# Wide gate products, 512-wide matmuls first, and three attention projection tiles placed among the gates

## The chip, the cores and the metric

The kernel runs on one core of a Trainium2 chip. The metric is the device time of one execution in microseconds. TensorE is called PE below, VectorE DVE, ScalarE ACT, GpSimd POOL, and SyncE, which issues most of the loads, SP. PE multiplies a stationary block of weights (128x128) with a moving block of up to 512 columns into a PSUM bank (128 x 512 fp32, eight banks).

## The reference

A two-layer encoder over 512 tokens of width 1024, in fp32. Per layer, with `h = rms_norm(x)`:

```python
z = h @ w_in[l]
q, k, v, cb, cc, cx, ga, gb = jnp.split(z, splits, axis=-1)
y_attn = band_attention(q, k, v, attn_sink[l]) @ w_attn_proj[l]
y_conv = (cb * short_conv(cc * cx, conv_w[l])) @ w_conv_proj[l]
mix = (jax.nn.sigmoid(ga) * y_attn + jax.nn.sigmoid(gb) * y_conv) @ w_out[l]
x = x + rms_norm(mix, g_post_mix[l])
h = rms_norm(x, g_pre_ffn[l])
f = (jax.nn.silu(h @ w_gate[l]) * (h @ w_up[l])) @ w_down[l]
x = x + rms_norm(f, g_post_ffn[l])
```

The change touches the gates `ga`, `gb` (two 1024x1024 products with h), the two projections that they weigh, the merge, and the order of matmuls in the gate and up products of the feed-forward block (FFN, 2816 wide).

## The kernel before, in words

**Precision.** Each fp32 operand is split into a high part (a cast to fp32r on ACT) and a low part (source minus high part, a subtraction on DVE). A product is the sum of three matmuls, high by low, low by high, high by high (`mm3`, L181 to L184). Some splits go "by DMA" instead (`split_by_dma`, L134): ACT writes the high part and the negated high part, and a DMA issued by POOL adds the source to it, so DVE does nothing.

**Stages of a layer**, in the order in which PE runs them: the value, key and query projections with the attention's pieces, interleaved with the conv branch; the conv projection (8 tiles, L856); the attention projection (8 tiles of 24 matmuls 512 wide, L933 to L938); the gates; w_out (`down`, L275, 8 blocks of k, five of them kept for the last pass); the FFN's gate and up products; w_down.

**Pairs.** Gates and FFN products are computed by `Pair` (L416): two output tiles (weights w0, w1, 1024 x 128 each) times the whole h, as 7 products of half size (a Strassen and Winograd scheme) instead of 8. A product p has four k steps. Its weight block is a sum of halves of the two weight tiles, made by DVE and then split (`prep`, L439). Its moving operand is one of seven sums of quarters of h, 256 columns high part and 256 low part, side by side. In the narrow form a k step is `mm3` with three 256-wide matmuls. In the wide form (`wide`, L502 and L506) a k step is one 512-wide matmul, high weights by both parts at once, and one 256-wide, low weights by the high part; the high-by-low sum then lies in the second half of the bank and is added when the bank is read (`total` L536, `plus` L544, and L528). Before the change all gates and the first five FFN pairs are narrow, and the other 17 FFN pairs are wide.

**What sets the order.** `orders` (L558) makes the list of (pair, product); `run_pairs` (L595) walks it, asking for the weights of the next 10 entries, making the operands of the next 5 (`AHEAD`) and those that go by DMA of the next 8 (`FAR`). Each engine runs its own instructions in order, and SP issues its loads in order, each when its destination is free. Buffers are taken in rotation: 22 slots of 4 KB per partition (`unit`, tag u4: second weight tiles, q, kept results, sums of h), 3 raw tiles (first weight tiles), 8 `hl` tiles (split weights), 6 each of t4 and t2, 8 PSUM banks.

**Gates.** `Gates.first` (L914) applies the sigmoid and multiplies by the attention's projection `ya`; `Gates.second` (L918) does the other gate with the conv projection `yc`, adds both, and splits the sum for w_out at once (L924 to L926). `yc` is kept in u4 slots from the conv projection on (L858 to L861), as is half of `ya`.

## Time and profile before

| what | value |
|---|---|
| median of 3 runs | 1645.69 us (1645.08 to 1647.68) |
| the profiled execution | 1645.89 us |
| its span | 1644.1 us, 25284 instructions |
| mean granted TensorE clock | 0.999 |
| attention projection, layer 0 | 312.7 to 356.3 us |
| gates, layer 0 | 356.3 to about 437 us |
| wide FFN pairs, layer 0 | about 541.5 to 703.3 us |

The span is what the profiler saw from the first to the last instruction; the execution's own time is 1.8 us longer. Rows of groups and of the timeline name the source line, the engine, the operation, and the tiles out<-in without their buffer numbers, so `bank<-u,hl` is a matmul that reads a moving operand in a u4 slot and a split weight tile.

### The profile page before, as it was taken

The page shows a single profiled execution, that of the slowest core. Times are in us where ns is not written, and L with a number is a line of the kernel's source. Part 1 is how long each engine was busy: PE and PEld are TensorE (multiplying, and loading weights), DVE is VectorE, ACT ScalarE, POOL GpSimd, SP SyncE. Part 2 cuts the span into 40 slices and gives each one's busy share as a digit, 9 for nine tenths or more (in the row PEclk, how much of TensorE's full clock was granted, in tenths as well). Part 3 has the DMA queues.
Part 4 walks back from the last instruction along what each step waited for, and adds up shares of the span by engine and source line. Part 5 has one row for each costly group of instructions (what it writes and reads, how often), then busy time and mean ns, then how long its engine had stood idle before and what let it go on. Part 6 is the DMA issues. An engine that isn't in the chain of part 4 may idle for free. (4 is left out here: it accounts for less than half of the span.)

```text
span 1644.1 us, 25284 instructions
## 1 busy us (share of the span) xinstructions
PE 1632.1 (99%) x9119; PEld 1422.5 (87%) x9119; DVE 1258.4 (77%) x2563; ACT 984.3 (60%) x2102; POOL 159.0 (10%) x222
## 2 busy tenths in 40 slices
PE   9999999999999999999999999999999999999998
PEld 8888888889989888888898888888998898888886
DVE  6978876749769999964469788766696799999442
ACT  5566666547657677743346676664575677777331
POOL 0000000000013222200000000000010332222000
PEclk9999999999999999999999999999999999999999
DMA  6322222245575766734413222223457657666332
GB/s 210 91 77 78 64 78 77 84 119 127 166 208 113 161 155 162 182 117 142 149 57 103 78 78 77 78 67 88 102 143 211 170 125 170 159 157 164 103 115 77
DMA packets 264541, 200.58 MB, mean 122 GB/s; under 512 B 7216, under 2 KB 238688, under 8 KB 264416
## 3 DMA queue, kind: packets, MB, share of 16 engines
q1 hardware_dynamic: 246240, 171.70, 35.4%
q0 software_dynamic: 17600, 26.22, 9.6%
q8 instruction: 71, 1.16, 0.3%
q10 hardware_dynamic: 576, 1.05, 0.2%
q14 instruction: 54, 0.44, 0.1%
HBM read 164.34 MB, written 8.39 MB: 105 GB/s over the span
## 5 line engine op out<-in xcount | busy, mean ns | idle before, releaser
L131 ACT CAST hl<-raw 128x512 fp32r<-128x512 f32 x362 | 220.9, 620 | 237.3 <-PE bank L184 181.9
L132 DVE TENSOR_TENSOR hl<-raw,hl 128x512 fp32r<-128x512 f32 x362 | 244.6, 688 | 154.4 <-ACT hl L131 154.0
L182 PE MATMUL bank<-h,hl 128*128 128x512 f32 (+1 forms) x992 | 340.1, 343 | 2.2 <-DVE h L214 2.2
L183 PE MATMUL bank<-h,hl 128*128 128x512 f32 (+1 forms) x992 | 336.5, 339 | 0.0
L184 PE MATMUL bank<-h,hl 128*128 128x512 f32 (+1 forms) x992 | 336.1, 339 | 0.0
L182 PEld LDWEIGHTS bank<-h,hl 128*128 128x128 f32 x992 | 188.3, 190 | 21.3 <-DVE h L214 3.5
L184 PEld LDWEIGHTS bank<-h,hl 128*128 128x128 f32 x992 | 188.1, 190 | 20.8
L183 PEld LDWEIGHTS bank<-h,hl 128*128 128x128 f32 x992 | 188.3, 190 | 17.6
L502 PE MATMUL bank<-h,hl 128*128 128x512 f32 x544 | 195.4, 399 | 0.0
L182 PE MATMUL bank<-u,hl 128*128 128x256 f32 (+1 forms) x568 | 189.4, 334 | 0.0
L184 PE MATMUL bank<-u,hl 128*128 128x256 f32 (+1 forms) x568 | 188.2, 331 | 0.0
L183 PE MATMUL bank<-u,hl 128*128 128x256 f32 (+1 forms) x568 | 188.1, 331 | 0.0
L132 DVE TENSOR_TENSOR hl<-t,hl 128x512 fp32r<-128x512 f32 x240 | 165.9, 695 | 18.8 <-ACT hl L131 17.6
L131 ACT CAST hl<-t 128x512 fp32r<-128x512 f32 x240 | 147.8, 621 | 33.5 <-DVE t L452 13.9
L506 PE MATMUL bank<-h,hl 128*128 128x256 f32 x544 | 152.8, 281 | 0.0
L502 PE MATMUL bank<-u,hl 128*128 128x512 f32 x408 | 147.3, 399 | 0.0
L502 PEld LDWEIGHTS bank<-h,hl 128*128 128x128 f32 x544 | 102.2, 188 | 25.2
L183 PE MATMUL bank<-hl,u 128*128 128x512 f32 x304 | 118.3, 389 | 0.0
L184 PE MATMUL bank<-hl,u 128*128 128x512 f32 x304 | 118.3, 389 | 0.0
L184 PEld LDWEIGHTS bank<-u,hl 128*128 128x128 f32 x568 | 107.9, 190 | 10.2
L182 PE MATMUL bank<-hl,u 128*128 128x512 f32 x304 | 116.6, 390 | 0.0
L182 PEld LDWEIGHTS bank<-u,hl 128*128 128x128 f32 x568 | 107.9, 190 | 10.0
(155 smaller groups left out, 3195.7 us busy)
## 6 DMA issues: line engine op xcount, KB each, us to landing
raw<-in_w_in_dram SPq DMA_DIRECT2D x88, 512.0 KB, 3.8
u<-in_w_up_dram SPq DMA_DIRECT2D x44, 512.0 KB, 6.7
raw<-in_w_down_dram SPq DMA_DIRECT2D x44, 512.0 KB, 3.4
raw<-in_w_gate_dram SPq DMA_DIRECT2D x40, 512.0 KB, 4.1
hl<-u POOLq DMA_DIRECT2D x58, 256.0 KB, 4.3
hl<-raw POOLq DMA_DIRECT2D x34, 256.0 KB, 3.7
raw<-in_w_conv_proj_dram SPq DMA_DIRECT2D x16, 512.0 KB, 3.7
raw<-in_w_attn_proj_dram SPq DMA_DIRECT2D x16, 512.0 KB, 3.8
```

Source lines behind the costliest of these rows:

```text
L131: nc.scalar.copy(h, raw)
L132: eng.tensor_tensor(out=lo, in0=raw, in1=h.bitcast(F32), op=ALU.subtract)
L182: nc.tensor.matmul(acc, wh, xl, start=first, stop=False, skip_group_check=goes_on)
L183: nc.tensor.matmul(acc, wl, xh, start=False, stop=False, skip_group_check=goes_on)
L184: nc.tensor.matmul(acc, wh, xh, start=False, stop=last, skip_group_check=goes_on)
L502: nc.tensor.matmul(acc.rearrange("p (a t) -> p a t", a=2), hl[:, 0, k], x, start=new and k == 0, stop=False, skip_group_check=True,)
L506: nc.tensor.matmul(acc[:, :TH], hl[:, 1, k], x[:, 0], start=False, stop=k == KH - 1, skip_group_check=True)
```

## The change

Five edits:

1. In a wide product all four 512-wide matmuls come first, then the four 256-wide. This holds for the wide FFN pairs and for the gates.
2. The gates are wide, and the weights of products 4, 2 and 1 are split by DMA (before: of product 4 alone).
3. The first five tiles of the attention projection stay ahead of the gates; tiles 5, 6 and 7 come before entries 20, 32 and 44 of the gates' list, as objects of a class `Projected` that count as two tiles in the look-ahead.
4. The conv projection's result goes to DRAM (8 stores of 256 KB a layer) and is loaded back in four loads of 512 KB, each issued at product 2 of an even gate.
5. From the third gate on, the merged result is kept in fp32 and split when w_out needs it.

Core of the diff:

```diff
         def product(self, p):
...
             acc = self.b if p == 2 else self.c if p in (5, 3) else self.a
             hl, op, new = self.hl.pop(p), self.r.op(p), p in (2, 1, 5)
+            wide = acc.shape[-1] == T
+            if wide:
+
+                for k in range(KH):
+                    nc.tensor.matmul(
+                        acc.rearrange("p (a t) -> p a t", a=2), hl[:, 0, k], row_of(op, k),
+                        start=new and k == 0, stop=False, skip_group_check=True,
+                    )
             for k in range(KH):
                 x = row_of(op, k)
-                if self.wide:
-                    nc.tensor.matmul(
-                        acc.rearrange("p (a t) -> p a t", a=2), hl[:, 0, k], x,
-                        start=new and k == 0, stop=False, skip_group_check=True,
-                    )
+                if wide:
                     nc.tensor.matmul(
                         acc[:, :TH], hl[:, 1, k], x[:, 0], start=False, stop=k == KH - 1, skip_group_check=True
                     )
...
-            for j, q in seq[n : n + FAR]:
-                if q in pairs[j].by_dma:
-                    pairs[j].prep(q)
-            for j, q in seq[n : n + AHEAD]:
-                pairs[j].prep(q)
+            for far in (True, False):
+                left = FAR if far else AHEAD
+                for j, q in seq[n : n + FAR]:
+                    left -= pairs[j].tiles
+                    if left < 0:
+                        break
+                    if not far or q in pairs[j].by_dma:
+                        pairs[j].prep(q)
             pairs[i].product(p)
...
+    merge_seq = []
+    for n, item in enumerate(orders(KT, 2, 3)):
+        tiles = range(5) if n == 0 else [5 + (n - 20) // 12] if n >= 20 and (n - 20) % 12 == 0 else []
+        merge_seq += [(KT + m, 0) for m in tiles if m < KT] + [item]
...
         def conv_proj(m):
             acc = yield from gemm_steps(a["w_conv_proj"][l], m * P, lambda k, part: cy[k][:, part])
-            if m % 2 == 0:
-                held["yc"] = unit([P, 2, T], F32)
-            yc[m] = held["yc"][:, m % 2]
-            nc.scalar.copy(yc[m], acc)
+            y = t2([P, T])
+            nc.scalar.copy(y, acc)
+            nc.sync.dma_start(ycd[l][:, m], y)
...
+        class Projected:
+            by_dma, tiles = (), 2
...
+            def product(self, p):
+                m = self.m
+                if m % 2 == 0:
+                    held["ya"] = unit([P, 2, T], F32)
+                ya[m] = held["ya"][:, m % 2]
+                acc = bank()
+                for k in range(KT):
+                    mm3(acc, self.hl(0, k), self.hl(1, k), qs[k][:, 0], qs[k][:, 1], k == 0, k == KT - 1)
+                nc.scalar.copy(ya[m], acc)
+
+        def parts_of(x):
+            u = unit([P, 2, T])
+            split_to(u[:, 0], u[:, 1], x)
+            return u[:, 0], u[:, 1]
+
         class Gates(Pair):
-            by_dma = (4,)
+            by_dma, wide = (4, 2, 1), True
+
+            def product(self, p):
+                super().product(p)
+                m = self.m
+                if p == 2 and m % 2 == 0:
+                    u = unit([P, 2, T], F32)
+                    nc.sync.dma_start(u, ycd[l][:, m : m + 2])
+                    yc[m], yc[m + 1] = u[:, 0], u[:, 1]
...
                 nc.vector.tensor_tensor(out=out, in0=out, in1=yc[m], op=ALU.mult)
-                nc.vector.tensor_tensor(out=out, in0=out, in1=self.out0, op=ALU.add)
-                u = unit([P, 2, T])
-                split_to(u[:, 0], u[:, 1], out)
-                mix[m] = u
+                if m < SOON:
+                    nc.vector.tensor_tensor(out=out, in0=out, in1=self.out0, op=ALU.add)
+                    mix[m] = parts_of(out)
+                    return
+                if (m - SOON) % 2 == 0:
+                    held["mix"] = unit([P, 2, T], F32)
+                mix[m] = held["mix"][:, (m - SOON) % 2]
+                nc.vector.tensor_tensor(out=mix[m], in0=out, in1=self.out0, op=ALU.add)
...
-        run_pairs(gates, gate_seq)
+        run_pairs(gates + [Projected(m) for m in range(KT)], merge_seq)
...
             down(
-                a["w_out"][l], KT, 5, lambda k: (mix[k][:, 0], mix[k][:, 1]), after_mix,
+                a["w_out"][l], KT, 5, lambda k: mix[k] if k < SOON else parts_of(mix[k]), after_mix,
```

Three places in the engines' orders, in layer 0. PE, at the start of the gates before: the last three matmuls of the attention projection's eighth tile, then the first product's twelve narrow matmuls, of which the first k steps are shown.

```order
L182 MATMUL bank_3520<-u_18_2098,hl_3517 128x512
L183 MATMUL bank_3520<-u_18_2098,hl_3517 128x512
L184 MATMUL bank_3520<-u_18_2098,hl_3517 128x512
L182 MATMUL bank_3572<-h_86,hl_3554 128x256
L183 MATMUL bank_3572<-h_86,hl_3554 128x256
L184 MATMUL bank_3572<-h_86,hl_3554 128x256
```

PE now, at entry 20 of the gates' list: a whole product (a moving operand in two u4 slots, so two rows of two matmuls for each width), and behind it the beginning of the projection's sixth tile (tile 5), which reads q from the u4 slots 6, 7, 8 and so on.

```order
L501 MATMUL bank_3719<-u_24_3267,hl_3734 128x512 x2
L501 MATMUL bank_3719<-u_25_3268,hl_3734 128x512 x2
L508 MATMUL bank_3719<-u_24_3267,hl_3734 128x256 x2
L508 MATMUL bank_3719<-u_25_3268,hl_3734 128x256 x2
L184 MATMUL bank_3824<-u_6_547,hl_3763 128x512
L185 MATMUL bank_3824<-u_6_547,hl_3763 128x512
L186 MATMUL bank_3824<-u_6_547,hl_3763 128x512
```

What was a row of three 256-wide matmuls for each k step is now four 512-wide and then four 256-wide, and the projection's tiles lie between gate products.

SP, the last loads for the gates, before: weights from w_in into raw tiles and u4 slots, with the first blocks of w_out behind and between them.

```order
L429 DMA raw_4135<-in_w_in_dram 128x8x128
L429 DMA raw_4269<-in_w_in_dram 128x8x128
L429 DMA u_42_4085<-in_w_in_dram 128x8x128
L429 DMA u_44_4219<-in_w_in_dram 128x8x128
L172 DMA raw_4633<-in_w_out_dram 128x1024
L429 DMA u_46_4353<-in_w_in_dram 128x8x128
L172 DMA raw_4665<-in_w_out_dram 128x1024
```

SP now, the same place:

```order
L960 DMA u_41_3969<-ycd_83 128x1024
L432 DMA u_42_3989<-in_w_in_dram 128x8x128
L149 DMA raw_4142<-in_w_attn_proj_dram 128x8x128
L432 DMA u_44_4128<-in_w_in_dram 128x8x128
L432 DMA raw_4179<-in_w_in_dram 128x8x128
L174 DMA raw_4504<-in_w_out_dram 128x1024
L960 DMA u_46_4215<-ycd_83 128x1024
L432 DMA u_47_4257<-in_w_in_dram 128x8x128
L174 DMA raw_4536<-in_w_out_dram 128x1024
```

Two loads of the conv projection from DRAM (`ycd`) and the weights of the last projection tile have come between; `u_47` is the second weight tile of the last gate, `u_42` and `u_44` those of gates 5 and 6.

DVE, where the last gate's second weights are first used, now: additions that make weight blocks (L457), low parts (L134) and evictions of banks (L542 to L549, L531). `u_47` is read in the first row.

```order
L457 TENSOR_TENSOR t_102_4350<-u_47_4257 128x512
L457 TENSOR_TENSOR t_103_4351<-t_102_4350,raw_4179 128x512
L134 TENSOR_TENSOR hl_4353<-t_102_4350,hl_4353 128x512
L542 TENSOR_TENSOR t_87_4222<-bank_4221,t_87_4222 128x256
L134 TENSOR_TENSOR hl_4366<-t_103_4351,hl_4366 128x512
L457 TENSOR_TENSOR t_102_4350<-t_103_4351,raw_4179 128x512
L542 TENSOR_TENSOR t_86_4115<-bank_4114,t_86_4115 128x256
L457 TENSOR_TENSOR t_103_4351<-raw_4179,u_47_4257 128x512
L134 TENSOR_TENSOR hl_4400<-t_102_4350,hl_4400 128x512
L971 TENSOR_TENSOR t_86_4115<-t_86_4115,u_41_3969 128x512
```

Everything behind the first of these rows waits with it; the twentieth row of this stretch is the eviction (L531) of the bank that product 4 of gate 6 writes next. The split of the merged result, on DVE before among the last gates, now stands among w_out's own splits (L134), here its rows of now:

```order
L216 TENSOR_TENSOR u_53_4614<-u_45_4198,u_53_4614 128x512
L979 TENSOR_TENSOR u_48_4451<-t_88_4370 128x512
L134 TENSOR_TENSOR u_54_4619<-raw_4617,u_54_4619 128x512
L134 TENSOR_TENSOR u_55_4622<-raw_4617,u_55_4622 128x512
L216 TENSOR_TENSOR u_56_4625<-u_45_4198,u_56_4625 128x512
```

Six such splits a layer (L216) have moved there, each one subtraction on DVE and one cast on ACT.

More of the change, by code (lines that the diff above doesn't have):

```diff
@@ L125, in taps @@
         nc.vector.tensor_copy(cw.rearrange("p l j c -> p (l j c)"), pt[:, :rows])
+    ycd = [tc.dram_tile([P, KT, T], F32, name=f"ycd{i}") for i in range(DEPTH)]
     xd = [tc.dram_tile([T, D], F32, name=f"xd{i}") for i in range(2 * DEPTH - 1)]
@@ L419, in encoder @@
         wide = False
+        tiles = 1
         by_dma = ()
@@ L444, in prep @@
                 self.prep(6)
+            if p == 7:
+                self.prep(3)
             self.done.add(p)
@@ L478, in product @@
         def product(self, p):
[L481 to L491 removed]
+            if p == 2:
+                self.ab = bank()
+                self.b = self.ab if self.wide else self.ab[:, TH:]
             elif p == 1:
[L493 to L494 removed]
+                self.a = bank() if self.wide else self.ab[:, :TH]
                 self.v = t4([P, 4, TH])
                 self.out0, self.out1 = (self.v[:, i : i + 2].rearrange("p a t -> p (a t)") for i in (2, 0))
+            elif p == 5:
+                self.c = bank() if self.wide else bank()[:, :TH]
             acc = self.b if p == 2 else self.c if p in (5, 3) else self.a
             hl, op, new = self.hl.pop(p), self.r.op(p), p in (2, 1, 5)
+            wide = acc.shape[-1] == T
[5 more added lines that the diff above has]
+                    )
             for k in range(KH):
                 x = row_of(op, k)
[L501 to L505 removed]
+                if wide:
                     nc.tensor.matmul(
@@ L526, in product @@
             elif p == 7:
-                if self.wide:
-                    nc.vector.tensor_tensor(out=v1, in0=self.a[:, TH:], in1=v1, op=ALU.add)
-                nc.vector.scalar_tensor_tensor(v1, self.a[:, :TH], -1.0, v1, op0=ALU.mult, op1=ALU.subtract)
+                if wide:
+                    nc.vector.tensor_tensor(out=v1, in0=acc[:, TH:], in1=v1, op=ALU.add)
+                nc.vector.scalar_tensor_tensor(v1, acc[:, :TH], -1.0, v1, op0=ALU.mult, op1=ALU.subtract)
             elif p == 4:
-                if self.wide:
-                    self.total(v0, self.a)
+                if wide:
+                    self.total(v0, acc)
                     self.a = v0
@@ L536, in total @@
         def total(self, v, acc):
-            if self.wide:
+            if acc.shape[-1] == T:
                 nc.scalar.copy(v, acc[:, TH:])
@@ L545, in plus @@
             nc.vector.tensor_tensor(out=out, in0=acc[:, :TH], in1=x, op=ALU.add)
-            if self.wide:
+            if acc.shape[-1] == T:
                 nc.vector.tensor_tensor(out=out, in0=acc[:, TH:], in1=out, op=ALU.add)
@@ L568, in free @@
                 return False
-            return p == 1 or len(seq) - at[i, before] >= 3
+            return p == 1 or len(seq) - at[i, before] >= lag
         for i in range(early):
@@ L582, in orders @@
             )
-            if opened < n and (len(left) < 2 or pick is None):
+            if opened < n and (len(left) < (2 if opened == n - 1 else 2) or pick is None):
                 for p in (2, 1):
@@ L932, in encoder @@
         mixed.sums()
-        for m in range(KT):
-            acc = gemm(a["w_attn_proj"][l], m * P, lambda k, part: qs[k][:, part])
-            if m % 2 == 0:
-                held["ya"] = t4([P, 2, T]) if m < KT // 2 else unit([P, 2, T], F32)
-            ya[m] = held["ya"][:, m % 2]
-            nc.scalar.copy(ya[m], acc)
-        run_pairs(gates, gate_seq)
+        run_pairs(gates + [Projected(m) for m in range(KT)], merge_seq)
         r = Rights()
```

36 lines of the change are left out of this document (14 added, 22 removed).

## The prediction

> **What bounds the kernel now.** I read the page first: shares of the span, then the slices.
>
> ```profile
> span 1644.1 us, 25284 instructions
> PE 1632.1 (99%) x9119; PEld 1422.5 (87%) x9119; DVE 1258.4 (77%) x2563; ACT 984.3 (60%) x2102; POOL 159.0 (10%) x222
> PEclk9999999999999999999999999999999999999999
> ```
>
> PE is busy for 99% of the span at full clock. The waits of PE say how little of the rest is a wait between engines (columns: total us, times, longest us):
>
> ```profile
> PE bank L182 <- DVE h L214: 2.2, 2, 1.2
> PE bank L668 <- POOL ident masks.py:199: 1.4, 1, 1.4
> PE bank L251 <- DVE t L239: 1.2, 1, 1.2
> ```
>
> The 2.2 us are the two turns from w_out to the FFN, the others the start; the change touches none of them. So there is nothing to win but PE's own time, matmul by matmul, and everything to lose where PE is made to wait. The view by windows of layer 0 (from:to, length, then busy us of PE, PEld, DVE, ACT, POOL, then clock, DMA share, GB/s) shows the four stages: attention projection, gates, w_out, wide FFN pairs.
>
> ```profile
> 312.00:356.30 44.30, 44.30 (x197) 36.70 (x196) 22.09 (x34) 16.88 (x31) 0.00 (x0) 1.00 0.43 117
> 356.30:439.20 82.90, 82.90 (x683) 82.40 (x683) 74.16 (x130) 60.14 (x121) 7.07 (x8) 1.00 0.53 142
> 439.20:483.60 44.40, 43.34 (x200) 35.71 (x199) 27.52 (x48) 24.44 (x52) 5.06 (x8) 1.00 0.68 190
> 541.50:703.30 161.80, 161.80 (x920) 140.26 (x918) 157.94 (x327) 114.50 (x227) 39.41 (x47) 1.00 0.70 166
> ```
>
> PE never stops in the gates or in the wide pairs, and in the latter DVE is at 98%. Matmuls are pipelined, so the spacing of their starts, not their duration, is what each costs. The timeline (start, duration, then the instruction) gives it:
>
> ```profile
> 402.42 0.28 PE L182 MATMUL bank<-h,hl 128*128 128x256 f32 x1
> ...
> 408.18 0.28 PE L182 MATMUL bank<-u,hl 128*128 128x256 f32 x1
> ```
> ```profile
> 601.47 0.40 PE L502 MATMUL bank<-h,hl 128*128 128x512 f32 x1
> 601.70 0.28 PE L506 MATMUL bank<-h,hl 128*128 128x256 f32 x1
> 601.82 0.40 PE L502 MATMUL bank<-h,hl 128*128 128x512 f32 x1
> ...
> 611.36 0.40 PE L502 MATMUL bank<-h,hl 128*128 128x512 f32 x1
> ```
> ```profile
> 706.85 0.39 PE L183 MATMUL bank<-hl,u 128*128 128x512 f32 x1
> ...
> 791.88 0.39 PE L182 MATMUL bank<-u,u 128*128 128x512 f32 x1
> ```
> ```profile
> 86.51 0.39 PE L182 MATMUL bank<-h,hl 128*128 128x512 f32 x1
> ...
> 88.59 0.39 PE L182 MATMUL bank<-h,hl 128*128 128x512 f32 x1
> ```
> ```profile
> 356.35 0.28 PE L182 MATMUL bank<-h,hl 128*128 128x256 f32 x1
> ...
> 356.94 0.28 PE L184 MATMUL bank<-h,hl 128*128 128x256 f32 x1
> ```
>
> First: 48 narrow matmuls in 5.76 us, 120 ns each, so a narrow product (12 of them) costs 1440 ns. Second: seven wide products, 28 pairs, in 9.89 us: 353.2 ns a pair, 1413 ns a product. Third: 375 matmuls 512 wide in 85.03 us of w_down: 226.7 ns each when nothing else lies between. Fourth: nine 512-wide ones just behind narrower matmuls of the attention: 231 ns. Fifth: five 256-wide ones just behind 512-wide: 118 ns. A steady 512 and a steady 256 add up to 346.7 ns, so an alternating pair loses 6.5 ns.
>
> **Edits 1 and 2 on PE.** Let P be a wide product with its 512s first. The gates have 2 x 8 x 7 = 112 products, which go from 1440 to P; the wide FFN pairs have 2 x 17 x 7 = 238, from 1413 to P. If both widths ran at their steady rates, P = 4 x 226.7 + 4 x 120 = 1387 ns: 112 x 53 + 238 x 26 = 5.9 + 6.2 = 12.1 us. If the order does nothing (the 6.5 ns could come from the moving operand, which in a wide product is two separate rows of 256 and in w_down one row of 512; no row of this trace separates the two), P = 1413: 112 x 27 = 3.0 us and nothing in the FFN. I take the rows behind a change of width, since with four of a kind the width changes every fourth matmul: 4 x 231 + 4 x 118.5 = 1398, rounded to 1400 ns: 112 x 40 + 238 x 13 = 4.5 + 3.1 = **7.6 us**.
>
> The Trainium skill, TensorE: Matmul & The Clock Gate, section "Back-to-back issue gap", gives a spacing of N / 2.4 GHz plus about 2.5 ns whatever stands ahead. By that a narrow product would take 12 x 109.2 = 1310 ns and a wide one 4 x 325 = 1300 in either order, so the gates would gain 112 x 10 ns = 1.1 us and the FFN nothing. This trace differs: 120 and 226.7 ns are 13.3 ns over N / 2.4, for both widths, and a pair in alternation costs more than the sum.
>
> **The other engines in the merge.** What the wide gates add, by groups of the gates' window (count | busy us, mean ns of one):
>
> ```profile
> L132 DVE TENSOR_TENSOR hl<-t,hl 128x512 fp32r<-128x512 f32 x31 | 21.0, 686 | 4.1 <-ACT hl L131 4.1
> L452 DVE TENSOR_TENSOR t<-t,raw 128x512 f32<-128x512 f32 x14 | 9.6, 688 | 0.2
> L529 DVE SCALAR_TENSOR_TENSOR t<-bank,t 128x256 f32<-128x256 f32 x8 | 3.3, 419 | 0.2 <-PE bank L184 0.2
> L214 DVE TENSOR_TENSOR u<-t,u 128x512 fp32r<-128x512 f32 x7 | 4.8, 687 | 0.3
> L131 ACT CAST hl<-raw 128x512 fp32r<-128x512 f32 x18 | 11.0, 619 | 2.7 <-PE bank L184 2.1 <-ACT hl L131 0.5
> L542 ACT COPY t<-bank 128x256 f32<-128x256 f32 x24 | 8.9, 371 | 7.1 <-PE bank L184 6.9
> L137 ACT ACTIVATE hl<-u 128x512 fp32r<-128x512 f32 x8 | 5.1, 633 | 0.0
> L938 ACT COPY u<-bank 128x512 f32<-128x512 f32 x1 | 0.6, 586 | 4.3 <-PE bank L184 4.3
> ```
>
> A gate has seven more additions out of banks on DVE (four in `total`, two in `plus`, one at product 7), 7 x 0.42 = 2.9 us, and two splits fewer, -1.4. Eight gates: +12.4 us. The six merged splits leave (-4.1), the splits of three projection tiles come (+4.1). DVE then has 74.2 + 12.4 = 86.6 us of work in a stage of 82.9 - 4.5 + 3 x 24 x 226.7 ns (16.3) = 94.7 us: 91%, against 89% before. ACT: one more copy a gate (0.37) and two more negated parts (1.27), +13.1; -6 x 0.62 and +3 x (2 x 0.62 + 0.59) = +1.8; 75 us, 79%. POOL issues 24 DMAs instead of 8. So no engine passes PE over the stage. A gate alone does: its DVE work is 4 low parts, 4 sums and 3 merge steps of 0.69 us and 10 evictions of 0.42, less some 0.06 us overlap at each of 21, 10.4 us, against 7 x 1.40 = 9.8 on PE. The projection tiles, 5.44 us of PE with 1.4 us of DVE each, are what covers that 0.6 us a gate; without the cover it would be 8 x 0.6 = 4.8 us a layer. The FFN pairs already run the same bank scheme with DVE at 98% and PE without a pause, which speaks for the bank rotation.
>
> **Where PE may wait.** The loads, by the DMA view of the gates' window (KB each, median us to landing):
>
> ```profile
> raw<-in_w_in_dram SPq DMA_DIRECT2D x5, 512.0 KB, 3.9
> hl<-u POOLq DMA_DIRECT2D x8, 256.0 KB, 3.9
> u<-in_w_in_dram SPq DMA_DIRECT2D x4, 512.0 KB, 5.4
> t<-in_g_post_mix_dram SPq DMA_DIRECT2D x1, 512.0 KB, 7.0
> ```
>
> With the projection among the gates, q stays in its u4 slots to the end, so the last second-weight tiles get theirs late. The tightest is the last gate's (`u_47`): its slot is free when the sixth matmul of projection tile 7 has read it, 1.4 us into that tile, so it lands at 6.8 us. DVE then needs 20 rows up to the eviction that frees gate 6's bank: 11 of 0.69 and 9 of 0.42 less the overlaps, 10.1 us: 16.9. PE wants that bank after the rest of the tile and eight products, 5.4 + 8 x 1.40 = 16.6. Behind the late load wait, on SP, w_out's second and third blocks, and on DVE all evictions of gates 6 and 7. The wait is 0.3 us by the median and 1.9 with 7.0 us to landing; below nothing it cannot be, since PE has no pause here that could go. I take 0.7 us a layer, **1.4 us**, with ends of 0 and 4. The other loads come out ahead: a block split by DMA (3.9 us) is asked for up to eight products ahead, 11 us, and gate 5's weights have some 5 us to spare by the same count.
>
> **Edits 4 and 5.** The stores (8 x 256 KB) leave while the projection's first tiles run, where DMA is at 0.43; ACT makes the same copy as before, into another buffer. The four loads come back half a gate or more ahead of their use (8 x 0.69 us of DVE multiplies). SP issues twelve more DMAs a layer, in a queue that is not full. I cost this at nothing; if the cover is gone, a load is late by its own 5.4 us. The six splits move to w_out, where DVE has 27.5 of 44.4 us, +4.1: covered there by PE's 43.3; uncovered it would be those 4.1 us a layer.
>
> **The sum** against the profiled execution, 1645.89 us (0.2 above the median of the runs): 1645.9 - 7.6 + 1.4 = **1639.7 us**.
>
> **The rivals.**
>
> *The order of widths does nothing.* Then P = 1413, the gates gain 3.0 us, the FFN none, the waits stay: 1645.9 - 3.0 + 1.4 = 1644.3 us, no change that can be told. For it: two rows of 256 in one instruction may be what costs 6.5 ns. The skill's formula named above leads to the same place, 1645.9 - 1.1 + 1.4 = 1646.2 us. Against it: 231 and 118 ns behind a change of width, with operands of one row. Chance 0.20.
>
> *Both widths run steady* (P = 1387) and the late load hides: 1645.9 - 12.1 = 1633.8 us. Against it: DVE in the FFN has 157.9 us per 161.8, and 3.1 us less on PE would bring it to 99.5%. Chance 0.10.
>
> *DVE sets the pace of the merge.* The evictions of gate by gate fall behind (10.4 against 9.8 us), banks come free late, and the projection tiles don't give it back: 9.6 us over both layers, 1645.9 - 7.6 + 9.6 = 1647.9 us. Against it: the 91% above. Chance 0.07.
>
> *The full u4 slots stall SP.* SP takes its loads in order; the second weights of gate 5 (`u_42`) wait for a slot that DVE frees in gate 3, and behind them stands the load for projection tile 7. If DVE is late there by the 5 us that I count as spare, the tile's weights are exposed too: 3.9 us to land, 0.6 and 0.7 to split, 5.2 us, and the late `u_47` adds its 1.9: 7 us a layer, 1645.9 - 7.6 + 14.2 = 1652.5 us, slower. It decides from 5.5 us a layer on (7.6 gained plus 3.3 to be slower). For it: q held to the end, DVE near full. Against: five tiles of 27 us ahead of the gates, in which DVE can run ahead. Chance 0.08.
>
> **How the numbers follow.** The forecast has 0.55, the rivals as given. About 0.2%, 3.3 us, is what a measurement can tell from no change: faster is below 1642.4, slower above 1649.0. Faster: nine tenths of the forecast's 0.55 and the steady case, 0.60, and a third of the first rival, where the waits are nothing and a little of the order's gain comes through, 0.07: 0.67. Slower: the SP rival and some of the DVE one: 0.10. Same: 0.23. The range reaches from the steady case, 1633.8, to the first rival with the waits at their upper end of 4 us, 1645.9 - 3.0 + 4 = 1646.9, which leaves out the slower cases and little else.
>
> **What would show it.** In a wide product, starts 228 to 233 ns apart for the four 512s and 117 to 120 for the 256s, product 1400 ns: right; 236 and 117 as now: the first rival. The gates and the three tiles in 94.7 us with pauses of about 0.7 us before product 4 of gate 6 and none elsewhere: right; many small pauses released by DVE or ACT on banks: DVE sets the pace; a pause before projection tile 7, with its weights just landed: SP. A pause in the FFN released by DVE would say that DVE takes what PE gave. I am wrong if the spacing does not fall, or if waits in the merge exceed 4 us a layer.

## The result, and the profile after

The changed kernel takes 1654.59 us (median of 5 runs, 1651.96 to 1660.18) where the kernel before takes 1645.69 (1645.08 to 1647.68): 1.0055 times as long, 95% interval 1.0043 to 1.0066. It is slower by 8.9 us, and 15 us away from the forecast of 1639.7. The profiled execution took 1656.28 us. Its page begins:

```profile
span 1654.5 us, 24668 instructions
PE 1631.3 (99%) x8671; PEld 1401.8 (85%) x8671; DVE 1275.9 (77%) x2643; ACT 1001.1 (61%) x2150; POOL 186.8 (11%) x254
```

The 448 matmuls fewer are there (8671 for 9119), and the time is longer all the same. The waits of PE (total us, times, longest):

```profile
PE bank L501 <- DVE t L531: 6.0, 4, 2.1
PE bank L501 <- DVE t L542: 5.1, 5, 2.4
PE bank L184 <- DVE h L216: 2.1, 2, 1.5
```

The third row is the old turn into the FFN. The first two are new, 11.1 us in nine pauses (five in layer 0, four in layer 1): the first matmul of a gate product (L501) waits until DVE has evicted the bank that it writes (L531, L542). By windows, most of the gates of layer 0, and a short stretch behind one of the pauses:

```profile
342.00:437.50 95.50, 89.22 (x473) 76.29 (x473) 72.53 (x148) 61.15 (x128) 17.40 (x20) 0.98 0.72 163
...
412.59:416.00 3.41, 3.41 (x13) 2.94 (x13) 2.92 (x6) 3.35 (x8) 0.87 (x1) 0.50 0.00 0
```

DVE is busy for only 76% of this stage, in which PE waits for it, so it is not too slow over the stage: it is waiting itself. The share of the DMA engines has gone from 0.53 to 0.72. DVE's own waits from 312 to 445 us:

```profile
DVE t L457 <- DMA u<-in_w_in_dram: 16.9, 5, 6.3
DVE hl L134 <- ACT hl L133: 7.1, 7, 2.5
```

L457 is an addition that makes a weight block, and `u<-in_w_in` is the load of a gate's second weight tile. DVE stands still for 16.9 us in layer 0 for five of these eight loads. In the gates of the kernel before no row of this view is a load.

One pause from end to end, the longest. What SP issues, around 340 us:

```profile
339.56 0.37 SPq L432 DMA_DIRECT2D raw<-in_w_in_dram  x1
340.02 0.53 SPq L960 DMA_DIRECT2D u<-ycd  x1
340.65 0.38 SPq L432 DMA_DIRECT2D u<-in_w_in_dram  x1
343.66 0.37 SPq L149 DMA_DIRECT2D raw<-in_w_attn_proj_dram  x1
344.12 1.04 SPq L432 DMA_DIRECT2D u<-in_w_in_dram  x1
```

Five loads of 512 KB leave within 5 us: a gate's first weights, the conv projection, second weights, weights of a projection tile, second weights. DVE reaches the row that needs the last of them:

```profile
350.22 0.41 DVE L542 TENSOR_TENSOR t<-bank,t 128x256 f32<-128x256 f32 x1
354.10 0.69 DVE L457 TENSOR_TENSOR t<-u 128x512 f32<-128x512 f32 x1 [3.47 <-DMA u<-in_w_in_dram]
354.71 0.42 DVE L542 TENSOR_TENSOR t<-bank,t 128x256 f32<-128x256 f32 x1
```

It waits 3.47 us, and the eviction behind it (L542 at 354.71) needs nothing of that load. PE needs the eviction:

```profile
352.11 0.64 PE L508 MATMUL bank<-u,hl 128*128 128x256 f32 x4
355.18 1.21 PE L501 MATMUL bank<-h,hl 128*128 128x512 f32 x4 [2.43 <-DVE t L542]
```

The load issued at 344.12 landed at about 354, ten microseconds later. The DMA engines were full meanwhile; this is their busy share from 340 to 360 us, in tenths, in 40 slices of half a microsecond (9 is 90% or more):

```profile
DMA  0369999999999999999999999941599400049854
```

A late load comes again at 390 us, where SP has stood for seven microseconds between two loads of first weights (the x2 in the row), and then sends three more:

```profile
381.10 8.10 SPq L432 DMA_DIRECT2D raw<-in_w_in_dram  x2
389.30 1.01 SPq L960 DMA_DIRECT2D u<-ycd  x1
390.36 0.48 SPq L432 DMA_DIRECT2D u<-in_w_in_dram  x1
393.80 0.37 SPq L149 DMA_DIRECT2D raw<-in_w_attn_proj_dram  x1
```
```profile
401.37 0.69 DVE L457 TENSOR_TENSOR t<-u 128x512 f32<-128x512 f32 x1 [6.32 <-DMA u<-in_w_in_dram]
```

Eleven microseconds from issue to landing. PE has a projection tile to run meanwhile and pauses later, for 0.43 us at 407.84 and 2.13 us at 411.63, while DVE, which works without a gap from 401.37 on, is still behind. Seven of the nine pauses, 9.0 us, stand in this way behind a wait of DVE for second weights.

The other two, 1.14 us at 391.90 and 0.91 us in layer 1, begin on ACT, which runs its rows in order too (386.30 and 387.36 are ACT's, then DVE's and PE's):

```profile
386.30 0.62 ACT L138 CAST hl<-raw 128x512 fp32r<-128x512 f32 x1 [2.37 <-DMA raw<-in_w_in_dram]
387.36 0.35 ACT L541 COPY t<-bank 128x256 f32<-128x256 f32 x1
387.74 0.42 DVE L542 TENSOR_TENSOR t<-bank,t 128x256 f32<-128x256 f32 x1 [1.50 <-ACT t L541]
391.90 1.20 PE L501 MATMUL bank<-u,hl 128*128 128x512 f32 x4 [1.14 <-DVE t L542]
```

The cast for a split by DMA (L138) waits for a gate's first weights, a copy out of a bank (L541) stands behind it, and DVE's eviction waits for that copy. ACT's waits for first weights come to 10.2 us in layer 0; in the gates of the kernel before ACT has none.

The DMA view of 312 to 445 us gives the medians, and the line's own view the spread of all loads of gate weights there (in the kernel before they took 3.7 to 6.5 us):

```profile
u<-in_w_in_dram SPq DMA_DIRECT2D x8, 512.0 KB, 6.6
```
```profile
DMA to landing us min/median/max: 3.7/5.8/11.0
```

The spacing of the matmuls, last. A wide FFN product now:

```profile
600.24 1.09 PE L501 MATMUL bank<-h,hl 128*128 128x512 f32 x4
601.17 0.64 PE L508 MATMUL bank<-h,hl 128*128 128x256 f32 x4
...
603.05 1.09 PE L501 MATMUL bank<-h,hl 128*128 128x512 f32 x4
```

Four 512-wide in 0.93 us, 232.5 ns each, and two products in 2.81 us: 1405 ns a product. So PE gains 112 x 35 = 3.9 us in the gates and 238 x 8 = 1.9 us in the FFN, 5.8 us. From 1645.89 to 1656.28 that leaves 16.2 us to be lost. The nine pauses are 11.1 of them. Behind two of the pauses the clock was at half (0.50 in the window above), and the matmuls took longer:

```profile
412.69 1.06 PE L508 MATMUL bank<-u,hl 128*128 128x256 f32 x4
413.55 1.91 PE L501 MATMUL bank<-h,hl 128*128 128x512 f32 x4
415.26 0.98 PE L508 MATMUL bank<-h,hl 128*128 128x256 f32 x4
416.07 1.08 PE L501 MATMUL bank<-h,hl 128*128 128x512 f32 x4
```

From start to start 0.86 us where 0.48 is usual, 1.71 where 0.93 is, and 0.81 where 0.48 is: 1.5 us, and as much in layer 1, 3.0 in all. The first four 512s behind any of the pauses take 1.02 to 1.07 us instead of 0.93, 1.0 us for the nine. The other 1.1 us are not assigned to rows.

### The profile page after: what moved, and what is told of

Read it like the earlier page. It is cut to its first block, busy times and chain, and to the rows that moved or that the text cites. A ratio compares the mean times of both kernels' runs of the same rounds, so it can differ in the third digit from the quotient of the medians.

```text
span 1654.5 us, 24668 instructions
## 1 busy us (share of the span) xinstructions
PE 1631.3 (99%) x8671; PEld 1401.8 (85%) x8671; DVE 1275.9 (77%) x2643; ACT 1001.1 (61%) x2150; POOL 186.8 (11%) x254
## 3 DMA queue, kind: packets, MB, share of 16 engines
q0 software_dynamic: 22208, 34.61, 12.8%
## 4 chain that ended last, share of the span: by engine, by line
PE 65%; DMA 2%; DVE 2%; ACT 0%; issue 0%; POOL 0%; DVEq 0%; POOLq 0%; SPq 0%; ACTq 0%
PE bank L501 15%; PE bank L184 13%; PE bank L185 13%; PE bank L186 13%; PE bank L508 7%; DMA u<-in_w_in_dram 2%; PE bank L768 1%; PE bank L815 1%; PE bank L802 1%; DVE hl L134 0%; DMA raw<-in_w_in_dram 0%; PE bank L386 0%; DVE t L457 0%; PE bank L253 0%; DVE t L273 0%
## 5 line engine op out<-in xcount | busy, mean ns | idle before, releaser
L133 ACT CAST hl<-raw 128x512 fp32r<-128x512 f32 x330 | 200.6, 620 | 221.2 <-PE bank L186 171.3
L134 DVE TENSOR_TENSOR hl<-raw,hl 128x512 fp32r<-128x512 f32 x330 | 222.7, 687 | 132.2 <-ACT hl L133 131.8
L184 PE MATMUL bank<-h,hl 128*128 128x512 f32 (+1 forms) x736 | 267.6, 364 | 2.1 <-DVE h L216 2.1
L185 PE MATMUL bank<-h,hl 128*128 128x512 f32 (+1 forms) x736 | 264.1, 359 | 0.0
L186 PE MATMUL bank<-h,hl 128*128 128x512 f32 (+1 forms) x736 | 263.6, 358 | 0.0
L501 PE MATMUL bank<-h,hl 128*128 128x512 f32 x800 | 220.1, 397 | 2.6 <-DVE t L542 2.6
L134 DVE TENSOR_TENSOR hl<-t,hl 128x512 fp32r<-128x512 f32 x240 | 166.0, 694 | 9.9 <-ACT hl L133 8.7
L501 PE MATMUL bank<-u,hl 128*128 128x512 f32 x600 | 164.5, 396 | 8.6 <-DVE t L531 6.0
L184 PEld LDWEIGHTS bank<-h,hl 128*128 128x128 f32 x736 | 139.1, 189 | 20.8 <-DVE h L216 3.1
L186 PEld LDWEIGHTS bank<-h,hl 128*128 128x128 f32 x736 | 139.0, 189 | 20.9
L501 PEld LDWEIGHTS bank<-h,hl 128*128 128x128 f32 x800 | 138.2, 190 | 21.8 <-DVE t L542 3.0
L185 PEld LDWEIGHTS bank<-h,hl 128*128 128x128 f32 x736 | 139.2, 189 | 17.7
L508 PEld LDWEIGHTS bank<-h,hl 128*128 128x128 f32 x800 | 123.7, 190 | 17.2
L184 PE MATMUL bank<-u,hl 128*128 128x512 f32 (+1 forms) x376 | 135.2, 360 | 0.0
L186 PE MATMUL bank<-u,hl 128*128 128x512 f32 (+1 forms) x376 | 134.0, 356 | 0.0
L185 PE MATMUL bank<-u,hl 128*128 128x512 f32 (+1 forms) x376 | 133.9, 356 | 0.0
L508 PE MATMUL bank<-h,hl 128*128 128x256 f32 x800 | 127.9, 282 | 0.0
L501 PEld LDWEIGHTS bank<-u,hl 128*128 128x128 f32 x600 | 103.0, 189 | 24.5 <-DVE t L531 7.2
```

Source lines behind the costliest of these rows:

```text
L133: nc.scalar.copy(h, raw)
L134: eng.tensor_tensor(out=lo, in0=raw, in1=h.bitcast(F32), op=ALU.subtract)
L184: nc.tensor.matmul(acc, wh, xl, start=first, stop=False, skip_group_check=goes_on)
L185: nc.tensor.matmul(acc, wl, xh, start=False, stop=False, skip_group_check=goes_on)
L186: nc.tensor.matmul(acc, wh, xh, start=False, stop=last, skip_group_check=goes_on)
L501: nc.tensor.matmul(acc.rearrange("p (a t) -> p a t", a=2), hl[:, 0, k], row_of(op, k), start=new and k == 0, stop=False, skip_group_check= ...
```

## The experiments

Times are medians; each ratio, with its 95% interval, is to runs of the kernel before on the same chip.

**e1, edit 1 alone** (on the kernel before):

```diff
-            for k in range(KH):
-                x = row_of(op, k)
-                if self.wide:
-                    nc.tensor.matmul(
-                        acc.rearrange("p (a t) -> p a t", a=2), hl[:, 0, k], x,
+            if self.wide:
+                for k in range(KH):
+                    nc.tensor.matmul(
+                        acc.rearrange("p (a t) -> p a t", a=2), hl[:, 0, k], row_of(op, k),
                         start=new and k == 0, stop=False, skip_group_check=True,
                     )
+            for k in range(KH):
+                x = row_of(op, k)
+                if self.wide:
                     nc.tensor.matmul(
```

> The kernel before with edit 1 alone: in the 238 wide products of the FFN the four 512-wide matmuls come first. In the profile of the whole change a wide FFN product takes 1405 ns where it took 1413, and the 17 wide pairs of a layer 1.2 us less. Theory A (the gain in the FFN is the order alone, and all that is lost lies in the merge): 2.4 us faster, 1643.3 us, ratio 0.9985, no new wait. Rival B (the FFN gains because the rest of the change left DVE more room there): no difference, 1645.7 us.

1644.13 us against 1646.14, ratio 0.9992 (0.9983 to 1.0001). By the medians the gain is 2.0 us, near theory A, by the ratio 1.3, and the interval touches 1, so the time alone does not tell it from none. The rows do: seven wide products of the FFN start within 9.82 us (from 600.40 to 610.22), 1403 ns each, where they took 1413. The order of widths costs nothing by itself, so the loss lies in the merge.

**e2, all projection tiles first** (on the whole change):

```diff
+    gate_seq = orders(KT, 2, 3)
...
-        run_pairs(gates + [Projected(m) for m in range(KT)], merge_seq)
+        for m in range(KT):
+            acc = gemm(a["w_attn_proj"][l], m * P, lambda k, part: qs[k][:, part])
+            if m % 2 == 0:
+                held["ya"] = t4([P, 2, T]) if m < KT // 2 else unit([P, 2, T], F32)
+            ya[m] = held["ya"][:, m % 2]
+            nc.scalar.copy(ya[m], acc)
+        run_pairs(gates, gate_seq)
```

> The whole change without edit 3: all eight projection tiles ahead of the gates, in the loop of before, half of their results in t4 buffers. q and the raw tiles are then free before the gates. Theory A (the second weight tiles come late, because q holds the u4 slots and the projection's weights share the three raw tiles and SP's queue with the gates): the loads are in time, DVE waits for no load, and the time falls from about 1654.6 to near 1640 to 1645 us. Rival B (DVE is too slow for wide gates, 10.4 us a gate against 9.8 on PE, and the projection tiles among the gates are what covers it): DVE busy without a pause, PE waits on banks 4 to 5 us a layer, 1648 to 1650 us.

1673.43 us, ratio 1.0168 (1.0154 to 1.0182): both theories missed, since it is worse by 19 us than the whole change. The longest of its waits of PE, and two rows of its DMA view from 312 to 452 us:

```profile
PE bank L508 <- DMA hl<-raw: 11.6, 4, 5.3
```
```profile
u<-in_w_in_dram SPq DMA_DIRECT2D x8, 512.0 KB, 12.5
hl<-raw POOLq DMA_DIRECT2D x16, 256.0 KB, 7.3
```

The second weights take 12.5 us to land, the splits by DMA 7.3, and now PE waits for these splits themselves. Without the projection's tiles between them the gates ask for the same bytes in less time. So tiles among the gates don't cause the loss; with them it is 19 us smaller. That they thin out the loads is my reading; this run also keeps half of `ya` in other buffers.

**e3, the conv projection loaded back once:**

```diff
-                if p == 2 and m % 2 == 0:
+                if p == 2 and m == 0:
                     u = unit([P, 2, T], F32)
                     nc.sync.dma_start(u, ycd[l][:, m : m + 2])
-                    yc[m], yc[m + 1] = u[:, 0], u[:, 1]
+                    for i in range(KT):
+                        yc[i] = u[:, i % 2]
```

> The whole change, but the conv projection is loaded back once a layer and this one tile pair serves all gates: three loads of 512 KB and three u4 slots fewer a layer, at the price that six of the eight output tiles of the merge use the wrong part of the conv projection. Theory A (bursts: these loads stand in SP's queue and share the DMA engines with the second weights, 7 to 11 us to landing against 5.4 before): most of the 16 us of new waits go, 1643 us or less. Rival B (the queue is held by the waits for raw tiles, whatever stands behind): a part of the waits stays, 1650 us or more.

1645.15 us, ratio 0.9997 (0.9988 to 1.0007): 9.4 us of the loss are gone with three loads and three slots a layer. Nearer to theory A than to B; some 4 to 5 us of waits stay.

**e4, second weights issued by POOL:**

```diff
+            eng = nc.gpsimd if n == 1 and isinstance(self, Gates) else nc.sync
-            nc.sync.dma_start(
+            eng.dma_start(
```

> The whole change, but the gates' second weight tiles are issued by POOL instead of SP, so that they don't stand behind SP's waits for raw tiles. Theory A (head of the line on SP): the second weights leave earlier, DVE's 16.9 us of waits for them in layer 0 shrink to a few, the time falls by 8 us or more, to 1646 us or less. Rival B (their u4 slots come free late, or the DMA engines are full): they land as late as before, 1652 us or more.

1656.63 us, ratio 1.0065 (1.0052 to 1.0079): no better, rival B. DVE's waits for these loads in layer 0 become a little shorter, and the loads land no sooner (a median of 6.5 us against 6.6):

```profile
DVE t L458 <- DMA u<-in_w_in_dram: 12.6, 4, 5.0
```

So waits at the head of SP's queue alone are not the cause, as far as this run shows: on POOL's queue these loads stand behind the splits by DMA instead, and the kernel has a new wait of 4.1 us at the projection's tiles.

**e5, the conv projection loaded back in small** (64 KB instead of 512, same slots, nearly the same order):

```diff
-                    nc.sync.dma_start(u, ycd[l][:, m : m + 2])
-                    yc[m], yc[m + 1] = u[:, 0], u[:, 1]
+                    nc.sync.dma_start(u[:, 0, :P], ycd[l][:, m, :P])
+                    yc[m] = yc[m + 1] = u[:, 0, :P].unsqueeze(1).broadcast_to((P, NT, P))
...
```

> The whole change, with the four loads of the conv projection a layer cut from 512 to 64 KB: 128 columns of an even tile serve, repeated, all columns of two output tiles, so that the merge uses wrong conv data. The u4 slots and the places in SP's queue stay (two second-weight loads move one place forward). Theory A (traffic: these loads share the DMA engines with the second weights): as with one load a layer, about 1645 us, the second weights in 5 to 6 us to landing. Rival B (the three slots and waits that the single load saved): near the whole change, 1652 us or more.

1641.42 us, ratio 0.9971 (0.9959 to 0.9982): theory A, by more than it said. Thirteen of the 16 us go with 1.75 MB a layer. The waits of PE on DVE's evictions shrink from 11.1 us to one row:

```profile
PE bank L501 <- DVE t L531: 1.2, 3, 0.7
```

So it is not their slots. Whether it is their bytes alone this run does not show: in each layer two second-weight loads have also moved a place forward, and the one that left at 344.12 us in the whole change, and cost PE 2.43 us, leaves at 341.02 here.

**e6, the conv projection loaded back later:**

```diff
-                if p == 2 and m % 2 == 0:
+                if p == 6 and m % 2 == 0:
```

> The whole change, with each load of the conv projection issued at product 6 of the even gate instead of product 2: the same traffic and slots, but for the later gates it stands behind the second weights in SP's queue instead of ahead of them. Theory A (what hurts is the burst in which it comes just ahead of the second weights): 4 to 9 us less than the whole change, 1646 to 1650 us. Rival B (the sum of traffic and slots, wherever it stands): 1653 us or more.

1647.93 us, ratio 1.0010 (1.0000 to 1.0020), 6.7 us better than the whole change: theory A. The same bytes hurt about half as much behind the second weights as ahead of them; here the order of the second weights' loads themselves is that of the whole change.

**e7, only product 4 split by DMA:**

```diff
-            by_dma, wide = (4, 2, 1), True
+            by_dma, wide = (4,), True
```

> The whole change, with only product 4 of a gate split by DMA, as before: 16 POOL DMAs of 256 KB a layer fewer, and 16 subtractions of 0.69 us a layer more on DVE (11 us, 1.25 us a gate after overlap). Theory A (traffic and raw tiles held by these DMAs make the loads late): DVE waits less for loads, and the time falls or stays, 1648 to 1654 us. Rival B (DVE sets the pace): 11.7 us a gate on DVE against 9.8 on PE, 10 us or so longer, 1660 us or more, with DVE busy.

1643.48 us, ratio 0.9982 (0.9973 to 0.9991): 11 us better, although DVE has 11 us of work a layer more. Theory A in direction, beyond it in size; rival B is out. In layer 0, 312 to 440 us, DVE is busy for 112 of 128 us and its waits for second weights have shrunk to a quarter; the loads land in a median of 5.6 us:

```profile
DVE t L457 <- DMA u<-in_w_in_dram: 4.2, 3, 1.8
```

At the place that cost PE 2.43 us in the whole change, DVE's rows are now these:

```profile
351.70 0.42 DVE L542 TENSOR_TENSOR t<-bank,t 128x256 f32<-128x256 f32 x1
352.72 0.69 DVE L457 TENSOR_TENSOR t<-u 128x512 f32<-128x512 f32 x1 [0.60 <-DMA u<-in_w_in_dram]
353.33 0.42 DVE L547 TENSOR_TENSOR t<-bank,t 128x256 f32<-128x256 f32 x1
```

The load lands at 352.7 instead of 354.1, and with more of DVE's own work in the order an eviction (L542) that stood behind the waiting row stands ahead of it. PE has no pause there. ACT's waits for first weights in the gates, 10.2 us in layer 0 of the whole change, are gone too. (The profiled execution, 1641.75 us, was the fastest of ten.)

**e8, edits 1 and wide gates alone** (on the kernel before; the diff is that of e1 and):

```diff
-            by_dma = (4,)
+            by_dma, wide = (4,), True
```

> The kernel before with the gates wide and the 512-wide matmuls first, and nothing else of the change: projection ahead of the gates, conv projection kept in SBUF, splits of the merged result among the gates, only product 4 split by DMA. PE gains 2.4 us in the FFN and 3.9 us in the gates. By the groups of before DVE has 74.2 us of work in the gates' window of layer 0 and gets 2.9 us a gate more, 97.6 us in 81 us. Theory A (wide gates alone overload DVE, which is what the other edits are for): 10 us a layer lost after a head start of some 7 us, about 1660 us, with DVE busy and PE waiting on banks. Rival B (the wait is only for loads, which are as before here): 1640 us.

1675.23 us (two runs), ratio 1.0175 (1.0155 to 1.0196): theory A, by 15 us more than it said. Here DVE is the bound, busy for 93.6 of 100 us while PE waits for it (the window of the gates, and the first two of PE's waits):

```profile
356.00:456.00 100.00, 88.41 (x478) 74.44 (x478) 93.56 (x188) 62.53 (x131) 7.08 (x8) 1.00 0.46 118
```
```profile
PE bank L501 <- DVE t L542: 9.1, 7, 2.0
PE bank L501 <- DVE t L531: 6.7, 3, 2.9
```

Compared with e7, this lacks edits 3, 4 and 5: 32 us lie between.

**e9, both remedies** (e6 and e7 together):

> The whole change with both remedies: only product 4 of a gate split by DMA, and the conv projection loaded back at product 6. PE alone would give 1645.9 - 2.4 - 3.9 = 1639.6 us; with product 4 alone by DMA 2.1 us of waits were left in the merges and 0.6 us more at a turn into the FFN. Theory A (the second weights late behind other DMA traffic are all that is left): less than 1.5 us of waits, 1641 to 1642.5 us, the fastest so far. Rival B (what is left is DVE's pace, 88% busy there): no better than 1643.5 us.

1639.39 us (1638.88 to 1641.79), ratio 0.9958 (0.9945 to 0.9972): the fastest of all, 6.3 us faster than the kernel before and 15 faster than the change. Of PE's waits on DVE's evictions this is left:

```profile
PE bank L501 <- DVE t L542: 1.2, 2, 0.7
```

Its profiled span is 1639.7 us, 4.4 below that of before; PE's 5.8 us less these 1.2 give 4.6.

**e10, four raw tiles and 21 u4 slots:**

```diff
-        return up.tile(shape, dtype, tag="u4", bufs=22, name=nm("u4"))
+        return up.tile(shape, dtype, tag="u4", bufs=21, name=nm("u4"))
...
-        return wp.tile([P, 1024], F32, tag="raw", bufs=3, name=nm("raw"))
+        return wp.tile([P, 1024], F32, tag="raw", bufs=4, name=nm("raw"))
```

> The whole change with four raw tiles instead of three and 21 u4 slots instead of 22, since there is no room for more. The traffic stays. Theory A (traffic: the second weights are slow to land among other transfers): no better than the whole change, 1652 us or more. Rival B (the splits by DMA of products 2 and 1 hold the raw tiles longer, SP waits for a raw tile, and what stands behind leaves late and together): several us better, 1650 us or less.

1690.26 us, ratio 1.0270 (1.0256 to 1.0285). It is 36 us slower than the whole change, and DVE waits 31.8 us for second weights in layer 0, for all eight of them. It does not separate the two theories: a slot was taken away and a raw tile given, and which of the two costs the 36 us is not shown. I take it to be the slot.

**e11, narrow gates in the new arrangement:**

```diff
-            by_dma, wide = (4, 2, 1), True
+            by_dma, wide = (4,), False
```

> The whole change with narrow gates and only product 4 split by DMA: the new arrangement of the merge without the wide gates, the FFN with its 512-wide matmuls first. PE has 112 products of 1440 ns where the wide ones take 1405, 3.9 us more, and DVE seven additions a gate fewer. Theory A (PE sets the end in this arrangement, and the loads are in time): 1643.5 + 3.9 less some of its 2 us of waits, 1645.5 to 1647.5 us. Rival B (wide gates bring nothing, since their evictions cost in waits what the matmuls save): 1643.5 us or less.

1645.31 us, ratio 0.9996 (0.9987 to 1.0005), just below the band of theory A: 1.8 us above e7. The profiled spans lie further apart, 1643.4 and 1639.9 us, with 1.7 us of waits on evictions in each, but e7's profiled execution was its fastest and e11's near its median, so the medians are the better measure. The new arrangement brings nothing without the wide gates, and the wide gates bring 1.8 us by the medians, of PE's 3.9; the two intervals overlap.

**e12, idle copies of split tiles added to e7** (against the whole change):

```diff
+    scr = [tc.dram_tile([P, 2 * KT, T], F32, name=f"scr{i}") for i in range(DEPTH)]
...
-            by_dma, wide = (4, 2, 1), True
+            by_dma, wide = (4,), True
+
+            def prep(self, p):
+                first = p not in self.done
+                super().prep(p)
+                if first and p in (2, 1):
+                    nc.gpsimd.dma_start(
+                        out=scr[l][:, 2 * self.m + p - 1].rearrange("p (k c) -> p k c", c=P),
+                        in_=self.hl[p][:, 0].bitcast(F32),
+                    )
```

> The kernel of e7 (only product 4 split by DMA, 1643.5 us) with 16 idle transfers a layer added on POOL's queue: when the weights of product 2 or 1 of a gate have been split, 256 KB of the split tile are copied to a scratch place in DRAM that nothing reads. They stand where the splits by DMA of the whole change stood, in size and number, but hold no raw tile, and the order of DVE, ACT and SP is that of e7. Theory A (traffic slows the second weights): most of what e7 gained over the whole change is lost again, 1649 us or more, with u<-in_w_in landing later than 5.6 us. Rival B (the splits by DMA hurt because they hold raw tiles and so the head of SP's queue, not by traffic): within 1.5 us of e7, 1645 us or less.

1643.92 us, ratio 0.9986 (0.9975 to 0.9997): 0.4 us over e7, rival B's number. The second weights land in a median of 6.5 us in layer 0, where e7 has 5.6 and the whole change 6.6, and by the medians it costs next to nothing. The profiled execution has 4.0 us of waits on evictions, against 1.7 in e7's:

```profile
PE bank L502 <- DVE t L532: 2.4, 2, 2.1
...
PE bank L502 <- DVE t L543: 1.6, 2, 1.1
```

**e13, a look-ahead of four in the merge:**

```diff
-                left = FAR if far else AHEAD
+                left = FAR if far else ahead
...
-        run_pairs(gates + [Projected(m) for m in range(KT)], merge_seq)
+        run_pairs(gates + [Projected(m) for m in range(KT)], merge_seq, ahead=4)
```

> The whole change with a look-ahead of four entries instead of five for making the weight blocks in the merge: the loads, their traffic, the splits by DMA and POOL's order are the same, but on DVE the additions that need a second weight tile stand later among the evictions of banks. Theory A (the order on DVE: a row that waits for a late load stands ahead of evictions that PE needs): the same late loads, but several us less of waits on PE, 1651 us or less. Rival B (the loads are late by themselves, whatever stands behind them; four entries only leave less time to make a block): 1654 us or more.

1651.10 us, ratio 1.0029 (1.0018 to 1.0041), 3.5 us better than the whole change, at the edge of theory A's band. PE's waits on evictions are 6.1 us where they were 11.1 (in an execution of 1649.27 us, among the fastest); DVE still waits 12.8 us for the loads in layer 0.

The loads did not stay quite the same: as in e5, the second weights of 344.12 us leave at 341.1, ahead of the projection tile's. So the 3.5 us are not those of DVE's order alone.

**e14, idle copies of raw tiles added to e7** (as e12, with `in_` the half of the raw tile that the product uses):

> The kernel of e7 with 16 idle transfers a layer on POOL's queue that copy the half of a raw tile that product 2 or 1 uses to a scratch place in DRAM. They hold the raw tile and add the traffic of the splits by DMA, and the order of DVE, ACT, SP and PE stays that of e7. Theory A (what the splits by DMA cost is the raw tile held, or traffic): 1648 us or more. Rival B (neither: what they change is the order on DVE and ACT, which stays here): within 1.5 us of e7, 1645 us or less.

1646.02 us, ratio 1.0000 (0.9990 to 1.0009): 2.5 us over e7, between the two theories. PE's waits on evictions come back by half, 5.9 us:

```profile
PE bank L502 <- DVE t L532: 4.3, 2, 2.1
PE bank L502 <- DVE t L543: 1.6, 1, 1.6
```

**What follows.** Most of the pauses of PE, 9.0 of 11.1 us, come from rows on DVE that wait for second weights while evictions stand behind them, and the rest from rows on ACT that wait for first weights; that is in the trace. Two of the change's edits make them: the loads of the conv projection, by their bytes and their place (e3, e5, e6), and the splits by DMA of products 2 and 1 (e7); with both mended all but 1.2 us are gone (e9). They are not additive: e5 alone takes away 13 us, e7 alone 11, of some 16. How the splits by DMA do it is not settled. Idle traffic of the same number and size costs 0.4 us, and 2.5 when it reads the raw tiles, so neither traffic nor held raw tiles account for 11. What else e7 changes is the order on DVE and ACT, with ACT's waits for first weights, and when each load is issued: around 390 us the four loads that leave SP within 5 us in the whole change (388.83 to 393.80) leave over 9 us in e7 (382.85 to 392.31). ACT's waits are not enough by themselves: e5 has 9.0 us of them in layer 0 and next to no pauses. e13 moves both the order and one load a layer, for 3.5 us. No run changes the order on DVE and ACT and nothing else.

## Why the prediction was wrong

- **What bounds the kernel** was read rightly: nothing to win but PE's time, everything to lose where PE waits. Both happened.
- **Edits 1 and 2 on PE** failed in size only. The term was 7.6 us with P = 1400 ns; P measured 1405, and the term 5.8. I had taken 231 ns from nine 512s behind a change of width; the first four of such a run take 232.5. The first rival (the order does nothing, P = 1413) is out by these rows and those of e1. The formula that was put beside it is, by that section of the Trainium skill (TensorE: Matmul & The Clock Gate, "Back-to-back issue gap"), the gap of an isolated matmul, not of a stream of weight loads and matmuls as here.
- **The other engines in the merge** was right about DVE. It was not the bound: with more work there (e7) the kernel is faster. That the projection's tiles help was right as well, and worth more than the 4.8 us a layer that I priced: e2, which lacks them alone, loses 19 us to the whole change. That what they cover is DVE's excess is shown in part: in e8 DVE is the bound, but e8 lacks edits 4 and 5 too (it loses 29 us to the kernel before), and in e2 the largest wait is for splits by DMA.
- **Where PE may wait** is the step that failed. I priced one late load, the last gate's, at 0.7 us a layer with an upper end of 4 us for both, and wrote that the other loads come out ahead. The wait that I priced is there, with the mechanism that I told: the last gate's load makes DVE wait 2.95 us at 429.96, its twentieth row from there is the eviction at 439.47, and PE pauses for 1.4 us; in layer 1 the same pause is 2.1 us. That is 3.5 us, inside my ends. But in layer 0 DVE waited for five of the eight second weights, and ACT for first weights; over both layers there were nine pauses where I had two, 11.1 us, and with what followed from them the whole came to about 16 us. Two things were missed. I took the time to landing from the kernel before (5.4 us), whose loads leave one or two at a time; here up to five leave together, and they took up to 11.0. And I worked out when a slot comes free, not when SP gets to the load, nor how many evictions stand behind each waiting row on DVE: I had named that queue for the last gate alone, though the same rows stand in every gate. ACT's order, with its casts that wait for first weights, I left out.
- **Edits 4 and 5 at nothing** failed too. I covered the four loads by an idle queue and priced the lost cover at one load's own 5.4 us. The cost was not in their own lateness but in that of the loads behind them: up to 13 us by e5. "POOL issues 24 DMAs instead of 8" I wrote down and did not price; it was worth 11 us by e7. The moved splits (edit 5) are named in no row of PE's waits.
- **The rivals.** The one that ended on the other side, full u4 slots and SP's queue, gave 1652.5 us, close to 1654.6, and had 0.08. Its parts were right in kind, late second weights and a full queue, but not its place: no projection tile was exposed, SP alone was not the cause (e4), and DVE's order was missing in it, so its number came close by luck. DVE's pace and the steady widths did not happen.
- **The range** ended at 1646.9, since its upper end took the same small waits. The trace of before could not show the bursts; the new order of SP could, and I read only its last rows.

## What to carry to other kernels

When a change adds loads to a queue, count how many leave together and price the last of them, not the median one of the old trace; the loads that suffer are those behind the added ones. On an engine that runs in order, look at what stands behind each row that waits for a load: an eviction there turns a late load into a pause of the engine that everything hangs on. Work moved from a compute engine to DMA is not free: here 11 us of DVE work a layer put back made the kernel 11 us faster, and its traffic alone does not explain that (e12), so look at what the move does to the order on the other engines.

## What the runs showed of the hardware

Behind a pause of 2.13 us the granted clock fell to 0.50 for 3.41 us, twice, from 412.59 us and in layer 1 from 1255.69, and not behind the longer pause of 2.43 us that ended at 355.18. So the length of the last pause does not decide it. The Trainium skill, TensorE: Matmul & The Clock Gate, section "What's actually happening", says that the clock follows the activity within a window of about 3.4 us that runs freely; a pause's place in such a window could be the difference. This case's traces agree. The two falls are 843.1 us apart, 247 times 3.4133 us. On a grid of that step, both pauses of 2.13 us lie whole within the stretch just before the fall, while the one of 2.43 us lies across a border, with at most 1.8 us in one stretch. Over all the traces here, leaving out the kernels' start and end, half clock followed each of the 17 stretches with 1.88 us or more of idle PE, and of those with 1.82 us or less only one (1.63 us, in e10).

The loads of the burst at 340 us landed in the order in which they left SP: those of 339.56, 340.02, 340.65, 343.66 and 344.12 us took 4.4, 5.3, 6.4, 6.3 and 9.9 us, where the loads of gate weights in the kernel before took 3.7 to 6.5. In e7, without two splits by DMA in the same stretch, the last of them took 8.4.
